# Attention's scores and P V as plain fp32 products, late q^T ranked behind the first heads, and new durations in the planner

## The chip, the cores and the metric

One core of a Trainium2 chip runs the whole model in one launch. The metric is device time in microseconds. Engines are named as in the profile: PE (matrix products; PEld is its weight load), DVE (vector), ACT (scalar, activations), POOL (gpsimd), and SP, the queue from which all DMAs of this kernel are issued.

## The reference, cut to what matters

A two-layer encoder on 512 tokens of width 1024, all fp32. Each sub-layer modulates its input with a shift and a scale that are linear in silu(c), runs a mixer or an MLP, and ends in a layer norm. The change lies in the first sub-layer, attention:

```python
h = x * (1.0 + scale) + shift
qkv = h @ w_in                      # 8 query heads, 2 key/value heads, 128 wide
q, k = rope(q[..., :32]), rope(k[..., :32])   # the first 32 of 128 features are rotated
# per block of 128 queries: keys of the block before, the own and the next
scores = einsum("bnqhgd,bnjhd->bnhgqj", qb, kb) * HEAD_DIM ** -0.5
m = max(max(scores), sink)
p = exp(scores - m)                 # outside the window: 0
probs = p / (sum(p) + exp(sink - m))
o = einsum("bnhgqj,bnjhd->bnqhgd", probs, vb)
y = o @ w_out
x = layer_norm(ALPHA * x + (1.0 + gate) * y)
```

After it come MLP 0, a recurrent block (depthwise convolution, gates, scans in both directions), and MLP 1, each with its layer norm.

## The kernel before, in words

**Products.** A large product is three products of a faster 32-bit type (fp32r): both operands are split into a high and a low part, and mm3 (L632) issues high x high, high x low, low x high. split (L639) makes the parts of an activation: ACT writes the high part, DVE subtracts it from the source (L642). Weights come by DMA as units of 128 x 1024 into one of four raw buffers and are split into one of six w buffers (conv_unit, L582). A few small products are not split: the transposes of P and of the layer norm's output, and the sums over partitions by a matrix of ones (L763), which are plain fp32 products.

**Stages.** k^T and q^T of six heads are accumulated over eight weight units (L1103 to L1114); rope (L990) evacuates them, four at a time: ACT packs the 32 rows that are rotated, each of the four tiles is split, DVE shuffles, multiplies and adds the packed rows, the result is split too, and two DMAs per head put the rotated rows back (L1009). V follows (L1129). Then the heads, in the order 0, 5, 1, 2, 3, 4, 6, 7 (L1017). For a head (L1166) there are four score blocks of 128 queries against 256 or 384 keys (L1175); DVE adds the mask and takes the maximum (L1178), ACT exponentiates, DVE or ACT divides (L1206), PE transposes P, the transposed P is split (put, L1198), and four products make P V (L1218), which is split again for the output projection. The q^T of heads 6 and 7 (48 products) is made after the heads at places 1 and 3 (LP, L1226). The output projection goes over two halves of 512 features (fh 0 and 1), out_tiles (L903); its first half starts as soon as heads are done, and with the second half each block of 128 tokens gets its layer norm (ln_block, L812) and is transposed for the MLP, whose first products (five units) take the first two blocks alone (NS, L680).

**Background.** The shifts, scales and gates of later sub-layers are matrix-vector products that DVE does as running sums, `acc = raw * sc + acc` over 128 x 1024 (gemv_tasks, L752), eight to a vector, with a plain product by ones at the end. Three vectors, 24 sums, fall into attention. Their weights go through the same four raw buffers, of which two are kept for them at least (keep_raw, L1117). Lines BV, BH and BG of the parameters say how many such tasks are recorded after a piece of V, after a head, and after a late head.

**What sets the order.** The kernel is first recorded as a list of operations. price (L293) gives each a duration, and schedule (L330) simulates five engines with these durations, always letting an engine take the ready operation of the lowest rank. The rank is the place in the recording plus an offset (later, L703, and the parameters CO, BO, PO, VO and others). The result is a fixed order of instructions on each engine, in which each engine then runs, waiting by semaphores. A duration in price has thus no effect but on the order.

The planner's price of PE (L303), of DVE (L308) and of DMA (L317 and L445), rope, attn and the parameter table are what the diff touches.

Of the kernel before, what the change touches and what calls it, by code (L numbers as in the profile page):

```python
# [233 lines left out]
class Program:  # L234
# [58 lines left out]
    def price(self, op, reads, writes):  # L293
# [7 lines left out]
        if op.eng == "tensor":  # L301
            op.nbytes = n * (reads[0].p1 - reads[0].p0) / 128
            passes = 1 if op.fn == "transpose" or op.kw["rhs"].ops[-1][0] == "b" else 4  # L303
            op.cost = 109 if op.fn == "transpose" else max(107 if passes == 1 else 213, passes * n * 0.4167 + 16)
# [3 lines left out]
        elif op.eng == "vector":  # L308
            if op.fn == "bn_stats":
                op.cost = reads[0].shape[1] * 1.042 + 68  # L310
            elif op.fn in ("tensor_scalar", "tensor_copy") and not ps:
                op.cost = n * 0.52 + 69 + 60 * aps
            else:
                op.cost = n * 1.042 + 65 + (60 if aps else 0)
        elif op.eng == "gpsimd":
            op.cost = {"memset": n * 0.85, "tensor_scalar": n * 3.4 + 105, "partition_all_reduce": n * 7.0}.get(op.fn, n * 2.105 + 147)
        else:  # L317
            p = w.shape[0]
            op.nbytes = p * n * 4
            op.cost = 480 if any(v.tile.kind == "dr" for v in reads + writes) or not reads else 650  # L320
# [9 lines left out]
    def schedule(self):  # L330
# [36 lines left out]
        while len(order) < total:  # L367
# [156 lines left out]
class Kernel:  # L524
# [127 lines left out]
    def fill(self):  # L652
# [16 lines left out]
        BH=4,  # L669
        BG=6,  # L670
# [15 lines left out]
        RP=60,  # L686
# [3 lines left out]
        LP=(1, 3),  # L690
        RE=0,
# [298 lines left out]
    def rope(self, heads):  # L990
# [5 lines left out]
        ph, pl = self.ex[10][:n, :], self.ex[11][:n, :]  # L996
# [5 lines left out]
        e = nc.gpsimd if self.P["RE"] else v  # L1002
        e.tensor_tensor(out=pk, in0=pk, in1=cos, op=ALU.mult)
# [3 lines left out]
        for i, (p, hi, lo) in enumerate(heads):  # L1007
            for dst, src in ((hi, self.ex[10]), (lo, self.ex[11])):
                nc.sync.dma_start(out=dst[0:32, :].bitcast(F32), in_=src[32 * i : 32 * i + 32, :])  # L1009

    def attn(self):
# [14 lines left out]
        def KTt(kv, lo, hi):  # L1026
            return self.HID(4 + kv, lo, hi)

        def V(t, lo, hi):
            return hid[12 + t][:, lo:hi].bitcast(F32R), hid[12 + t][:, 256 + lo : 256 + hi].bitcast(F32R)  # L1030

        def Q(h, lo, hi):
            if h == 5:
                return self.HID(3, lo, hi)
            a = self.ex[2 * (h % 6)], self.ex[2 * (h % 6) + 1]
# [505 lines left out]
```

## Time and profile before

| | |
|---|---|
| three runs | 1210.86, 1211.11, 1212.65 us (median 1211.11) |
| the profiled execution's own time | 1211.31 us |
| its span, first to last instruction | 1209.5 us |
| PE busy | 1142.6 us, 94% |
| DVE busy | 872.3 us, 72% |
| ACT busy | 528.5 us, 44% |
| PE's granted clock, mean | 0.974 |

A clock of 1.00 is 2.4 GHz; the lower of its two levels is 1.2 GHz, so a stretch with 0.50 ran at the lower one throughout. All operations of this kernel stand under one line, L476, since the planner issues them; so they are told apart by the names of their tiles: ps a PSUM bank, raw and w weights before and after the split, ht the transposed activations, hid and ex and xb and rows and acc working tiles. `rows<-raw,sc,rows` and `acc<-raw,sc,acc` are the running sums of the background. In the timeline a row merges instructions of one kind that follow each other; a start-to-start distance says how long the engine was held, which is a little less than an instruction's own duration.

### The profile page before, as it was taken

How to read it: one execution, taken by the hardware profiler on the slowest of the kernel's cores; microseconds unless marked ns; L12 is line 12 of the kernel's file. 1: busy time of each engine (PE TensorE's matmuls, PEld its weight loads, DVE VectorE, ACT ScalarE, POOL GpSimd, SP SyncE). 2: the span in 40 equal slices, each digit the busy share in tenths (PEclk: the TensorE clock that was granted, in tenths of full speed). 3: DMA queues.
4: the chain of work that ended last, by engine and by line, in shares of the span. 5: the costliest groups of instructions: out<-in, count | busy, mean ns of one | idle time of the engine just before them, and what ended most of it. 6: DMA issues, size and time to landing. Idle time of an engine off the chain costs nothing.

```text
span 1209.5 us, 14406 instructions
## 1 busy us (share of the span) xinstructions
PE 1142.6 (94%) x5332; PEld 942.0 (78%) x5332; DVE 872.3 (72%) x1303; ACT 528.5 (44%) x787; POOL 77.0 (6%) x47
## 2 busy tenths in 40 slices
PE   7977989999999899999999989979999999999996
PEld 5876858988888688887887877768888888888885
DVE  7899979978878885449958788689935444444447
ACT  4465654512322342324378889834531322322311
POOL 1000000022232220000000000000000000000004
PEclk9998999999999999999999989989999999999998
DMA  9866552367667753321333542442532323232201
GB/s 351 288 201 202 166 188 71 121 211 263 207 234 236 244 196 135 95 97 37 100 101 100 142 125 83 150 140 86 169 111 89 103 90 103 90 101 90 101 1 70
DMA packets 54140, 172.01 MB, mean 142 GB/s; under 512 B 7715, under 2 KB 8227, under 8 KB 54070
## 3 DMA queue, kind: packets, MB, share of 16 engines
q1 hardware_dynamic: 54070, 171.09, 43.1%
q8 instruction: 42, 0.69, 0.2%
q14 instruction: 28, 0.23, 0.1%
HBM read 160.56 MB, written 2.11 MB: 134 GB/s over the span
## 4 chain that ended last, share of the span: by engine, by line
PE 57%; DVE 20%; ACT 8%; DMA 8%; issue 5%; POOL 2%; SPq 1%; DVEq 0%; ACTq 0%; POOLq 0%
PE ps L476 57%; DVE ex L476 5%; DVE w L476 5%; DVE rows L476 4%; DMA raw<-in_adaw 3%; DVE xb L476 2%; ACT rows L476 2%; ACT w L476 2%; POOL ex L476 2%; DMA raw<-in_W 1%; DMA rows<-w 1%; DVE ht L476 1%; DVE acc L476 1%; ACT ex L476 1%; ACT L476 1%
## 5 line engine op out<-in xcount | busy, mean ns | idle before, releaser
L476 PE MATMUL ps<-ht,w 128*128 128x512 f32 (+1 forms) x2664 | 557.1, 371 | 6.3 <-ACT w L476 3.9
L476 PEld LDWEIGHTS ps<-ht,w 128*128 128x128 f32 x2664 | 464.2, 191 | 94.6 <-ACT w L476 4.3
L476 PE MATMUL ps<-w,hid 128*128 128x512 f32 (+1 forms) x1800 | 415.2, 390 | 0.0
L476 DVE TENSOR_TENSOR w<-raw,w 128x1024 fp32r<-128x1024 f32 x192 | 241.0, 1260 | 223.1 <-ACT w L476 220.7
L476 PEld LDWEIGHTS ps<-w,hid 128*128 128x128 f32 x1800 | 335.3, 188 | 72.0 <-DVE rows L476 0.2
L476 ACT CAST w<-raw 128x1024 fp32r<-128x1024 f32 x192 | 198.5, 1041 | 420.6 <-PE ps L476 305.2
L476 PE MATMUL ps<-w,ht 128*128 128x512 f32 (+1 forms) x336 | 76.0, 378 | 6.9 <-DVE w L476 3.6
L476 PEld LDWEIGHTS ps<-w,ht 128*128 128x128 f32 x336 | 58.4, 197 | 19.4 <-DVE w L476 4.1
L476 DVE SCALAR_TENSOR_TENSOR ex<-rows,ps 128x512 f32<-128x512 f32 (+1 forms) x81 | 53.3, 674 | 20.4 <-PE ps L476 20.4
L476 DVE SCALAR_TENSOR_TENSOR acc<-raw,sc,acc 128x1024 f32<-128x1024 f32 x40 | 52.8, 1320 | 16.4 <-DMA raw<-in_adaw 16.1
L476 DVE SCALAR_TENSOR_TENSOR rows<-raw,sc,rows 128x1024 f32<-128x1024 f32 x40 | 54.6, 1365 | 5.7 <-DMA raw<-in_adaw 5.5
L476 ACT ACTIVATE rows<-ps 128x512 f32<-128x512 f32 x66 | 39.2, 593 | 44.6 <-PE ps L476 41.7
L476 DVE TENSOR_TENSOR xb<-xb,ex 128x512 f32<-128x512 f32 (+1 forms) x81 | 55.9, 703 | 0.6
L476 POOL TENSOR_TENSOR ex<-xb,rows 128x512 f32<-128x512 f32 x5 | 6.8, 1375 | 750.7 <-ACT xb L476 750.7
L476 DVE TENSOR_TENSOR hid<-ex,hid 128x512 fp32r<-128x512 f32 x66 | 47.6, 722 | 5.3 <-ACT hid L476 0.7
L476 DVE TENSOR_TENSOR ex<-rows 128x512 f32<-128x512 f32 x64 | 46.0, 718 | 4.8 <-ACT rows L476 4.7
L476 ACT ACTIVATE hid<-rows 128x512 fp32r<-128x512 f32 x64 | 40.5, 633 | 1.9
L476 PE MATMUL ps<-ex,w 96*128 96x512 f32 x108 | 33.1, 464 | 7.7 <-ACT w L476 4.2
L476 PEld LDWEIGHTS ps<-ex,w 96*128 96x128 f32 x108 | 23.5, 223 | 15.7 <-ACT w L476 5.8
L476 DVE TENSOR_TENSOR rows<-rows,ex 128x512 f32<-128x512 f32 x32 | 21.4, 688 | 19.6 <-DMA rows<-rows 12.5
L476 ACT ACTIVATE xb<-xb,mv 128x512 f32<-128x512 f32 x29 | 22.2, 809 | 26.4 <-DVE mv L476 26.3
L476 ACT ACT_TABLE_LOAD x24 | 30.8, 1283 | 1.1 <-PEq L1533 0.7
(147 smaller groups left out, 819.3 us busy)
## 6 DMA issues: line engine op xcount, KB each, us to landing
raw<-in_W SPq DMA_DIRECT2D x184, 512.0 KB
raw<-in_adaw SPq DMA_DIRECT2D x80, 512.0 KB
ex<-in_ada0t SPq DMA_DIRECT2D x28, 256.0 KB
rows<-w SPq DMA_DIRECT2D x16, 192.0 KB
raw<-in_W SPq DMA_DIRECT2D x8, 288.0 KB
rows<-rows SPq DMA_DIRECT2D x36, 64.0 KB
xb<-in_xT SPq DMA_DIRECT2D x8, 256.0 KB
rows<-in_lnb SPq DMA_DIRECT2D x4, 512.0 KB
```

The lines of the kernel that those rows point to most:

```text
L476: op.ins = getattr(getattr(nc, op.eng), op.fn)(*args, **kw)
```

## The change

Scores and P V become one plain fp32 product each. q^T, k^T, V and the transposed P are no longer split but copied from PSUM, by ACT or DVE as the strings QE and PE say; the rotated rows are not split either, and one DMA per head puts them back instead of two. The q^T of heads 6 and 7 is recorded before all heads, with 200 added to its rank (QP), and the places LP are gone. Three background tasks are recorded after every head (BH). The P tiles of successive heads use two halves of the same buffers. The planner's prices change: a plain product counts its four passes as activity of PE, a scan costs 2.083 ns a column instead of 1.042, a DMA's issue is 600 ns for all, its data come at 330 bytes per ns instead of 360, and up to 5000 ns of them may be queued instead of 3000.

```diff
             passes = 1 if op.fn == "transpose" or op.kw["rhs"].ops[-1][0] == "b" else 4
-            op.nbytes = n * (reads[0].p1 - reads[0].p0) / 128
+            op.nbytes = passes * n * (reads[0].p1 - reads[0].p0) / 128
...
+            elif op.fn == "tensor_tensor_scan":
+                op.cost = n * 2.083 + 65
...
-            op.cost = 480 if any(v.tile.kind == "dr" for v in reads + writes) or not reads else 650
+            op.cost = 600
...
-                b = max(st + op.cost + 720, dma_free)
-                dma_free = b + op.nbytes / 360.0
-                now[e] = max(st + op.cost, dma_free - 3000)
-                op.end = dma_free
+                b = max(st + 1030, dma_free)
+                dma_free = b + op.nbytes / 330.0
+                now[e] = max(st + op.cost, dma_free - 5000)
+                op.end = dma_free + (30 if op.nbytes > 300000 else -230)
...
-        BH=4,
-        BG=6,
+        BH=3,
+        QE='aavavavava',
+        PE='ava',
...
+        VP=0,
+        QP=200,
-        LP=(1, 3),
...
-        for p, hi, lo in heads:
-            self.split(p[:, :], hi, lo)
+        for i, (p, dst) in enumerate(heads):
+            if how[i] == "a":
+                nc.scalar.copy(out=dst, in_=p[:, :])
+            else:
+                v.tensor_copy(out=dst, in_=p[:, :])
...
-        self.split(pk, ph.bitcast(F32R), pl.bitcast(F32R))
-        for i, (p, hi, lo) in enumerate(heads):
-            for dst, src in ((hi, self.ex[10]), (lo, self.ex[11])):
-                nc.sync.dma_start(out=dst[0:32, :].bitcast(F32), in_=src[32 * i : 32 * i + 32, :])
+        for i, (p, dst) in enumerate(heads):
+            nc.sync.dma_start(out=dst[0:32, :], in_=self.rows[4][32 * i : 32 * i + 32, 0:512])
...
-                self.split(p[:, 0:256], *V(t, 0, 256))
+                nc.scalar.copy(out=V(t, 0, 256), in_=p[:, 0:256])
...
+        self.nc.offset += self.P["QP"]
+        for n in range(2):
+            u = N_WQ + 2 + n
+            self.prep(u, ahead=2)
+            p = self.ps()
+            for k in range(KT):
+                self.mm3(p[:, :], self.W(u, k * 128, k * 128 + 128), self.HT(k), k == 0, k == KT - 1)
...
-                self.mm3(p[:, :n], Q(h, b * 128, b * 128 + 128), KTt(kv, lo, hi), True, True)
+                nc.tensor.matmul(p[:, :n], lhsT=Q(h, b * 128, b * 128 + 128), rhs=KTt(kv, lo, hi), start=True, stop=True)
...
-                    self.split(pj[j][:, :n], hi, lo)
+                    if self.P["PE"][min(j, 2)] == "a":
+                        nc.scalar.copy(out=PT(h, j, n), in_=pj[j][:, :n])
+                    else:
+                        v.tensor_copy(out=PT(h, j, n), in_=pj[j][:, :n])
...
-                self.mm3(o[:, q0 : q0 + cnt], V(j, kv * 128, kv * 128 + 128), PT(h, j, cnt), n == 0, n == 3)
+                nc.tensor.matmul(
+                    o[:, q0 : q0 + cnt], lhsT=V(j, kv * 128, kv * 128 + 128), rhs=PT(h, j, cnt), start=n == 0, stop=n == 3, skip_group_check=True
+                )
```

Because the planner rules on all engines, the order moves almost everywhere in attention. Three places matter. The rows are the program's, L476 (before) or L478 (after) being the line that issues everything, and a number behind a name telling tiles apart.

On PE, after V, before: the last score block of the first head (three products), then the late q^T of head 6 in one piece (w_93), and the next head's scores; the first transpose stands some 30 rows further on.

```order
L476 MATMUL ps_709<-hid_108,ex_527 128x256
L476 MATMUL ps_709<-hid_109,ex_527 128x256
L476 MATMUL ps_709<-hid_108,ex_536 128x256
L476 MATMUL ps_714<-ht,w_93 128x512 x24
L476 MATMUL ps_758<-hid_108,ex_532 128x256
L476 MATMUL ps_758<-hid_109,ex_532 128x256
```

The same place after: the scores of the first two heads and more stand ahead, one row to a block, and the late q^T is cut into pieces between which the first transposes (ident) stand.

```order
L478 MATMUL ps_723<-hid_109,ex_555 128x256
L478 MATMUL ps_726<-hid_108,ex_540 128x256
L478 MATMUL ps_733<-ht,w_93 128x512 x10
L478 MATMUL ps_756<-hid_108,ex_524 128x256
L478 MATMUL ps_760<-ident,xb_705 128x128
L478 MATMUL ps_733<-ht,w_93 128x512
L478 MATMUL ps_760<-ident,rows 128x128
L478 MATMUL ps_760<-ident,ex_81 128x128
```

So the 24 products of a late q^T moved from in front of the second head's scores into the time in which the first heads' softmax runs.

On DVE, at the end of the second head's score reductions, before: the sums of the background (raw, sc) stand between the small softmax operations (den, nm, rd) and the normalizations of the first head.

```order
L476 SCALAR_TENSOR_TENSOR rows<-raw_85,sc,rows 128x1024
L476 TENSOR_TENSOR den_796<-den_796,es_777 128x4
L476 TENSOR_SCALAR nm_826<-mx_788 128x4
L476 SCALAR_TENSOR_TENSOR rows<-raw_86,sc,rows 128x1024
L476 RECIPROCAL rd_835<-den_796 128x4
L476 SCALAR_TENSOR_TENSOR rows<-raw_87,sc,rows 128x1024
L476 TENSOR_SCALAR xb_732<-xb_732,rd_835 128x256
L476 TENSOR_SCALAR ex_81<-ex_81,rd_835 128x384
L476 TENSOR_TENSOR den_832<-den_832,es_830 128x4
L476 SCALAR_TENSOR_TENSOR rows<-raw_85,sc,rows 128x1024
L476 RECIPROCAL rd_856<-den_832 128x4
L476 TENSOR_TENSOR w_93<-raw_84,w_93 128x1024
```

The same place after; the COPY is a P tile out of PSUM.

```order
L478 TENSOR_SCALAR nm_731<-mx_716 128x4
L478 TENSOR_TENSOR den_729<-den_729,es_721 128x4
L478 RECIPROCAL rd_751<-den_729 128x4
L478 TENSOR_SCALAR xb_705<-xb_705,rd_751 128x256
L478 TENSOR_SCALAR ex_81<-ex_81,rd_751 128x384
L478 ISA xb_705,mx_778<-ps_688,rows,sinks 128x256
L478 ISA mx_778 128x1
L478 COPY xb_319<-ps_774 128x384
L478 TENSOR_TENSOR den_748<-den_748,es_744 128x4
```

The sums moved behind: four of the 24 stand before the first reduction, none between there and the fourth head's P copy, the others after it.

On DVE, around the last P V's split (ht from ps), before: the operations that build the layer norm's rows (rows from rows or acc, 128x1024) and the last splits, then the evacuation of the output projection (ex from rows, ps).

```order
L476 TENSOR_TENSOR w_91<-raw_84,w_91 128x1024
L476 SCALAR_TENSOR_TENSOR rows<-rows 128x1024
L476 TENSOR_TENSOR xb_879<-ps_1441,xb_879 128x384
L476 TENSOR_TENSOR rows<-acc_68,rows 128x1024
L476 TENSOR_TENSOR ht<-ps_1460,ht 128x512
L476 TENSOR_TENSOR ht<-ps_1477,ht 128x384
```

After, from the last split on:

```order
L478 TENSOR_TENSOR ht<-ps_1301,ht 128x512
L478 SCALAR_TENSOR_TENSOR ex_1326<-rows,ps_987 128x512
L478 SCALAR_TENSOR_TENSOR rows<-raw_85,sc,rows 128x1024
L478 SCALAR_TENSOR_TENSOR ex_1337<-rows,ps_993 128x512
L478 SCALAR_TENSOR_TENSOR rows<-raw_84,sc,rows 128x1024
L478 TENSOR_TENSOR xb_1306<-xb_1306,ex_1337 128x512
```

Four sums and all three row operations now stand behind the last split, among the evacuations; and on PE the eight transposes of the first block's layer norm, which stood among the output projection's last products, stand behind them all.

## Rows read from the trace of the kernel before

**Rows 1.** The page: PE's busy time, share of the span, instructions.

```profile
PE 1142.6 (94%) x5332; PEld 942.0 (78%) x5332; DVE 872.3 (72%) x1303; ACT 528.5 (44%) x787; POOL 77.0 (6%) x47
```

**Rows 2.** The table by stretches: attention in three, then the MLP's first products.

```profile
core 0: us, PE busy (x) PEld busy (x) DVE busy (x) ACT busy (x) POOL busy (x), PEclk, DMA share, GB/s
56.39:98.11 41.72, 29.69 (x188) 25.93 (x187) 38.06 (x71) 25.87 (x53) 0.00 (x0) 0.88 0.64 208
98.11:169.43 71.32, 64.82 (x331) 51.60 (x331) 61.56 (x133) 46.44 (x111) 2.46 (x4) 0.97 0.59 194
169.43:200.87 31.44, 29.36 (x133) 22.95 (x131) 28.13 (x59) 14.52 (x20) 0.00 (x0) 1.00 0.18 55
200.87:206.60 5.73, 5.73 (x35) 5.63 (x35) 5.73 (x14) 2.07 (x3) 0.00 (x0) 0.70 0.23 70
206.60:214.00 7.40, 7.40 (x65) 7.38 (x64) 7.40 (x16) 1.75 (x4) 0.00 (x0) 1.00 0.35 122
```

**Rows 3.** Timeline of PE: start, length, operation, idle before and its releaser.

```profile
59.11 11.07 PE L476 MATMUL ps<-w,ht 128*128 128x256 f32 x96
...
72.49 1.44 PE L476 MATMUL ps<-hid,ex 128*128 128x256 f32 x8 [1.72 <-DMA ex<-ex]
73.77 5.67 PE L476 MATMUL ps<-ht,w 128*128 128x512 f32 x24
...
88.56 0.48 PE L476 MATMUL ps<-ident,rows 128*128 128x128 f32 x1 [4.16 <-ACT rows L476]
...
98.11 3.86 PE L476 MATMUL ps<-xb,hid 128*128 128x512 f32 x12 [0.78 <-DVE mx L476]
...
169.43 2.04 PE L476 MATMUL ps<-w,ht 128*128 128x512 f32 x8
...
199.54 1.26 PE L476 MATMUL ps<-ident,ex 128*128 128x128 f32 x8 [1.40 <-DVE ex L476]
```

**Rows 4.** Timeline of DVE from the first head's reductions to the first P V.

```profile
78.84 0.16 DVE L476 TENSOR_SCALAR nm<-mx 128x4 f32<-128x4 f32 x1
...
83.49 1.28 DVE L476 SCALAR_TENSOR_TENSOR rows<-raw,sc,rows 128x1024 f32<-128x1024 f32 x1 [0.65 <-DMA raw<-in_adaw]
84.69 0.48 DVE L476 CUSTOM_DVE_ANT_0 xb<-ps,rows,sinks 128x256 f32<-128x256 f32 x1
...
92.32 1.20 DVE L476 TENSOR_TENSOR w<-raw,w 128x1024 fp32r<-128x1024 f32 x1
93.43 0.68 DVE L476 TENSOR_TENSOR xb<-ps,xb 128x512 fp32r<-128x512 f32 x1
94.03 1.28 DVE L476 SCALAR_TENSOR_TENSOR rows<-raw,sc,rows 128x1024 f32<-128x1024 f32 x1
...
95.49 0.42 DVE L476 TENSOR_SCALAR rows<-rows,rd 128x384 f32<-128x384 f32 x1
95.82 0.55 DVE L476 TENSOR_TENSOR xb<-ps,xb 128x384 fp32r<-128x384 f32 x1
96.28 1.28 DVE L476 SCALAR_TENSOR_TENSOR acc<-raw,sc,acc 128x1024 f32<-128x1024 f32 x1
```

**Rows 5.** Chain of waits in 76:100: start, length, what.

```profile
78.64 4.82 DMA raw<-in_adaw
...
86.40 4.54 DMA raw<-in_adaw
```

**Rows 6.** PE's weight loads of a plain fp32 product (sum over partitions).

```profile
102.37 0.19 PEld L476 LDWEIGHTS ps<-rows,ones 128*128 128x128 f32 x1 [0.27 <-DVE mx L476]
102.80 0.19 PEld L476 LDWEIGHTS ps<-rows,ones 128*128 128x128 f32 x1 [0.24 <-issue]
```

**Rows 7.** Timeline of DVE: the second block's layer norm output.

```profile
198.80 1.29 DVE L476 TENSOR_TENSOR ex<-ex,rows 128x512 f32<-128x512 f32 x2
```

**Rows 8.** The recurrent stage: one stretch, and its scans by form.

```profile
600.00:860.00 260.00, 243.62 (x1073) 197.55 (x1072) 208.69 (x308) 183.37 (x268) 0.00 (x0) 0.95 0.39 118
...
L476 DVE TENSOR_TENSOR_SCAN w<-rows 128x512 f32<-128x512 f32 x16 | 19.1, 1215 | 0.0
```

More of the change, by code (lines that the diff above doesn't have):

```diff
@@ L689 @@
         RO=0,
-        LP=(1, 3),
-        RE=0,
         KW=(0, 0, 1),
@@ L988, in late_consts, with rope @@
         nc.sync.dma_start(out=self.ex[12][:, 0:384], in_=I["mask"])
-    def rope(self, heads):
+    def rope(self, heads, how):
         nc, v = self.nc, self.nc.vector
@@ L1118, in attn @@
         self.modes = self.P["AM"]
-        qk = [(tiles[m], *(KTt(m, 0, 512) if m < 2 else Q(m - 2, 0, 512))) for m in range(8)]
-        self.rope(qk[:4])
-        self.rope(qk[4:])
+        qk = [(tiles[m], KTt(m, 0, 512) if m < 2 else Q(m - 2, 0, 512)) for m in range(8)]
+        self.rope(qk[:4], self.P["QE"][:4])
+        self.rope(qk[4:], self.P["QE"][4:8])
         accv, r = self.acc2, [a[:, :] for a in self.rows]
@@ L1135, in attn @@
             with self.later("VO"):
-                self.split(p[:, 0:256], *V(t, 0, 256))
+                nc.scalar.copy(out=V(t, 0, 256), in_=p[:, 0:256])
+        self.nc.offset -= self.P["VP"]
+        for t in range(TB):
             self.bg(self.P["BV"])
@@ L1139, in attn @@
         self.done(u + 1)
+        late = []
+        self.nc.offset += self.P["QP"]
[5 more added lines that the diff above has]
+                self.mm3(p[:, :], self.W(u, k * 128, k * 128 + 128), self.HT(k), k == 0, k == KT - 1)
+            self.done(u)
+            late.append((p, Q(6 + n, 0, 512)))
+        self.rope(late, self.P["QE"][8:])
+        self.nc.offset -= self.P["QP"]
         self.renew("xb", range(TB))
-        pt_at = [(0, 0, 512), (1, 0, 512), (2, 0, 384), (0, 256, 768)]
+        pt_at = [(0, 0), (1, 0), (2, 0), (0, 256)]
         pt_n = [256, 384, 384, 256]
@@ L1147, in PT @@
         def PT(h, j, n):
-            t, hi, lo = pt_at[j]
-            i = order.index(h)
-            if i > 3 and i % 2:
-                hi, lo = 4096 + t * 1024 + hi, 4096 + t * 1024 + lo
-                return self.ht[:, hi : hi + n].bitcast(F32R), self.ht[:, lo : lo + n].bitcast(F32R)
-            return self.xb[t][:, hi : hi + n].bitcast(F32R), self.xb[t][:, lo : lo + n].bitcast(F32R)
+            t, a = pt_at[j]
+            a += order.index(h) % 2 * 512
+            return self.xb[t][:, a : a + n]
         n_s = [0]
@@ L1222, in attn @@
         uo = N_WQ + 4
-        late, at = [], self.P["LP"]
-        for i, h in enumerate(order):
+        for h in order:
             head(h)
-            if i in at:
-                n = at.index(i)
-                u = N_WQ + 2 + n
-                self.prep(u, ahead=2)
-                p = self.ps()
-                for k in range(KT):
-                    self.mm3(p[:, :], self.W(u, k * 128, k * 128 + 128), self.HT(k), k == 0, k == KT - 1)
-                self.done(u)
-                late.append((p, *Q(6 + n, 0, 512)))
-            self.bg(self.P["BH" if i <= at[1] else "BG"])
-            if i == at[1]:
-                assert 4 * self.P["BV"] + (i + 1) * self.P["BH"] <= 20
-                with self.later("RP"):
-                    self.rope(late)
-                for half in range(2):
-                    nc.gpsimd.memset(self.ht[:, 5120 + half * 512 + 384 : 5120 + half * 512 + 512], 0.0)
+            self.bg(self.P["BH"])
         self.load_ln_rows(0)
@@ L1247, in attn @@
         self.renew("ex", range(10))
+        self.renew("hid", range(8, 16))
         self.flush_bg()
```

18 lines of the change are left out of this document (6 added, 12 removed).

## The prediction

> **What bounds the kernel now.** I read the page first: PE is busy for 94% of the span [rows 1], so a saving has to come from the few stretches in which PE waits. The table by stretches then shows where these are. In 56.39:98.11 us (V, the first scores, the first softmax) PE is busy for 29.69 of 41.72 us and DVE for 38.06; in 98.11:169.43 (the rest of the heads) PE for 64.82 and DVE for 61.56 of 71.32 us; in 169.43:200.87 (the rest of the output projection and the layer norm) PE for 29.36 and DVE for 28.13 of 31.44 us [rows 2]. So in attention DVE is as full as PE, and in its first third it is what PE waits for. The timeline of PE shows the holes: 4.16 us in front of the first transpose at 88.56, and the first P V product only at 98.11, 28 us after V was done [rows 3]. The timeline of DVE shows why: between the score reductions and the normalizations stand sums of the background matrix-vector work (raw times sc into rows or acc), 1.20 us each, and the split of P [rows 4]. The chain of waits adds a second reason: in 76:100 two of these sums wait 4.82 and 4.54 us for their 512 KB of raw weights [rows 5], because only two or three raw buffers circulate. What stands behind such a sum on DVE waits with it.
>
> **PE: what the plain products cost.** A plain fp32 product is not unknown here: the sums over partitions (rows, ones) are such products. Their weight loads stand 0.43 us apart and there are two to a product [rows 6], so 512 columns take 0.86 us, 1.68 ns a column. Three split passes take 3 x 11.07/96 us on 256 columns, 1.35 ns a column, and 3 x 5.67/24 on 512, at most 1.38 [rows 3]. A head has 256+384+384+256 = 1280 columns of scores and 512+384+256+256 = 1408 of P V; eight heads have 21,504. The change costs PE 21,504 x 0.30 to 0.37 ns = 6.5 to 8.0 us; I take 7.5. All of it is PE's own time; whether it lengthens the stage depends on the holes.
>
> **DVE: what goes.** Starts in [rows 4] give 0.60 us for a split of 512 columns (93.43 to 94.03), 0.46 for 384 (95.82 to 96.28), and by their ratio 0.34 for 256. Gone are 18 of 512 (ten q^T and k^T, one per head for P), 16 of 384 (two per head), 4 of 256 (V) and the three of the rotated rows (0.60): 10.8 + 7.4 + 1.4 + 1.8 = 21.4 us. New are DVE copies out of PSUM, 4 of 512 and 8 of 384. No copy of that kind is in the trace; the bounds are the split's price (2.4 + 3.7 = 6.1 us) and that of a one-input operation in SBUF, 0.33 us for 384 (95.49 to 95.82), 4.4 us in all. I take 6.1, the row that also reads PSUM. DVE loses 15.3 us. The Trainium skill (VectorE: DVE Perf Modes, Why PSUM operands drop a tier) says that an fp32 operation with a PSUM operand runs at one element per cycle, which speaks against hoping for the faster price; by it the sum would be this same 6.1 us, and no run so far shows it. ScalarE does one P copy less per head and six of ten q and k copies instead of ten casts; it was busy for 72 of 113 us [rows 2] and stays behind the other two. The rope writes halve from 20 small DMAs to 10, so q of head 0 arrives before V is done: the 1.7 us hole in front of the scores goes.
>
> **The order: the first four heads.** In the new DVE order no matrix-vector sum stands between the first score reduction and the fourth head's P copy (between the same points there were 13 before), and on PE the products of the late q^T stand in the hole after the scores. I walk through the new order with these prices. V ends at 70.2 as before. Scores of head 0 take 2.15 us and are reduced by 74.6. Before, 9.7 us passed from there (78.84, nm from mx) to the first transpose at 88.56, with three sums of 1.20 us and a wait of 0.65 in between [rows 3, 4]; without these it is 5.4 us, so the transposes start at 80 and the first P V at about 83 (98.11). From there PE is full: V 11.1, four heads at 2.15 + 2.37 us = 18.1, both late q^T 2 x 5.4 = 10.7 and 40 transposes at 0.13 = 5.2 [rows 3] make 45.1 us, so P V of the fourth head ends at 59.1 + 45.1 = 104. Of the 41.72 us up to the first P V, PE was idle for 12.0 [rows 2]: this is the cover under which the dearer products disappear; without it they cost their 7.5 us.
>
> **The order: the last four heads.** What DVE skipped early comes now: 16 sums between the fourth head's P copy and the last head's split. The last twelve of these run through two raw buffers alone (raw_84 and raw_85 in the order). One turn is a reload of 4.4 us [rows 5] and the sum's 1.20, 5.6 us for two sums. DVE needs about 15 us from 106 for two heads' reductions, the rope of the late heads (2.5), two weight splits (2.2) and three sums, plus some 2 us for its first reload, so the run of twelve sums begins at about 121; five turns later, at 149, its last pair starts, and the last head's split ends at 153, its P V at 151. PE alone could be there at 148 (before: 169.4): 59.1 + V 11.1 + eight heads 36.2 + late q^T 10.7 + 80 transposes 10.4 + 72 products of the output projection 17 + four sums over partitions 3.4 = 147.9. Bounds: 148 (PE never waits) and 158 (PE as idle as in 98.11:169.43, 6.5 us, and the walk too short by as much again).
>
> **The tail.** Before, 31.4 us passed from the last P V to the first MLP product at 200.87 [rows 2, 3]; PE had 28 us of output projection there, and the second block's layer norm ended at 200.0 [rows 7]. Now DVE has, between the last split and the same point, 32 operations of 512 columns (19.2 us), four sums that used to be done before (4.8), the three operations that build the layer norm's rows (two of them were done before) and four weight splits (7 x 1.11 = 7.8) and small ones (1.5): 33.3 us, and about 4 us of waits, for the last reloads (four loads of x and the norm's rows now stand in the same queue) and for the last sum's product, which PE has behind the second block's output products. So the second block is ready at 153 + 37.3 = 190.2 and the MLP starts at 191, while PE finished at 181 and waits for 8 us in two pieces. I add 0.5 for small waits: 191.5. The stage gains 200.87 - 191.5 = 9.4 us.
>
> **After it.** PE comes out of a wait of 4 to 5 us. Before, after 1.4 us of idle, its first 5.73 us ran at a clock of 0.70 [rows 2]; I add 1 us for 0.50 over the same stretch (5.73 x 0.20 = 1.1). The Trainium skill (TensorE: Matmul & The Clock Gate, HAM oscillation) says that each wait for data between bursts lets PE fall to the lower clock and that the next burst starts slow; the 0.70 agrees, and by that rule too the wait would cost about the same 1 us on top. Elsewhere the same instructions run in a slightly other order. The planner priced a scan at 512 x 1.042 + 65 = 598 ns; the trace has 1215 [rows 8], and the corrected formula gives 1131. In the recurrent stage, 600:860, PE is idle for 16.4 us [rows 8]. Its new order can win or lose there; nothing in the trace prices it, so the bounds are half of that idle time either way, 8 us; the MLP stretches are full and keep their length. I take a gain of 1.
>
> **Sum.** Profiled execution 1211.31 us (span 1209.5, 1.8 around it; 0.2 above the median of 1211.11): 1211.3 - 9.4 + 1 - 1 = 1202.
>
> **Rivals.**
> PE-bound to the end: the raw buffers keep up, the last P V ends at 148 and the tail is as short as before, MLP at 148 + 31.4 = 179.4: 1211.3 - 21.5 = 1190. For it: PE's sum. Against it: 4.4 us per reload in the chain of waits, and four more sums in the tail. Chance 0.13.
> The tail eats it: the waits behind the reloads are longer than in my walk, 6 to 8 us more, so that the MLP starts at 198 to 200: 1208 to 1211. For it: a walk leaves out small waits, and DVE was 88% busy in the heads before [rows 2]. Chance 0.13.
> Slower: the plain products decide. If the softmax chain (reduction, exponential, sum, normalization, transpose) and not DVE's load set the holes, they stay, and PE's 7.5 us go on top: 1219. It decides from the point where the first P V is not earlier than about 95. For it: PE was 91% busy in 98.11:169.43 [rows 2]. Against it: the waits in 76:100 are for DVE and the raw loads, and both go. Chance 0.11.
> That the orders elsewhere turn against it by more than 8 us I give 0.03 (no change).
>
> **The numbers.** The forecast has 0.60, its own range is 1196 to 1208. The range for 8 in 10 reaches into both neighbours: 1189 to 1212. What a measurement can tell from no change here is 0.2%, 2.4 us. Faster: 0.60 + 0.13 + 0.09 of the tail's case = 0.82; same: 0.04 + 0.03 = 0.07; slower 0.11.
>
> **What would show it.** In the profile after: the first transposes at about 80 and the first P V at about 83; DVE without matrix-vector sums from 73 to 104 and waiting for raw loads from 105 on; two PE instructions per score block, 0.43 us apart for 512 columns; the last P V at 151; PE idle twice before the first MLP product at 191.5; from there to the end of the span 1008 to 1009 us (before: 1209.5 - 200.87 = 1008.6). It is wrong if P V of the first head comes after 90, if PE has no idle time in front of the MLP, or if the stretch from the MLP's start to the end differs by more than 8 us.

## The result, and the profile after

The change takes 1199.61 us (median of 4 runs, 1197.29 to 1201.10) against 1210.98 (4 runs of the kernel before on the same chip): ratio 0.9902, 95% interval [0.9883, 0.9921]. Forecast 1202, faster. The profiled execution took 1198.96 us, its span 1197.2.

The page of the kernel after, its first line (before: [rows 1]):

```profile
PE 1138.4 (95%) x5268; PEld 931.5 (78%) x5268; DVE 858.1 (72%) x1274; ACT 523.1 (44%) x774; POOL 77.5 (6%) x45
```

The table by stretches of the kernel after: from V to the first P V, to the end of the last P V, to the first MLP product, and the first 5.67 us of the MLP. It answers to the same marks in [rows 2], which stand there at 98.11, 169.43 and 200.87; the first stretch there begins at 56.39, 2.7 us ahead of V.

```profile
59.90:89.87 29.97, 25.39 (x150) 21.18 (x149) 22.22 (x47) 17.87 (x40) 0.00 (x0) 0.94 0.60 192
89.87:157.69 67.82, 66.00 (x285) 46.68 (x284) 52.76 (x119) 39.65 (x100) 0.95 (x1) 1.00 0.52 162
157.69:197.93 40.24, 32.88 (x142) 25.21 (x140) 35.76 (x67) 20.23 (x26) 0.96 (x1) 0.97 0.52 175
197.93:203.60 5.67, 5.67 (x33) 5.67 (x33) 5.67 (x17) 2.41 (x4) 0.00 (x0) 0.62 0.27 82
```

Heads are dense now (PE 66.00 of 67.82 us), but the tail grew to 40.24, and of 11.7 us gained up to the last P V only 2.9 are left at the first MLP product. The whole of V to MLP, before and after:

```profile
59.11:200.87 141.76, 121.16 (x637) 98.24 (x635) 125.53 (x258) 84.16 (x180) 2.46 (x4) 0.95 0.52 168
```
```profile
59.90:197.93 138.03, 124.28 (x574) 93.08 (x572) 110.74 (x232) 77.74 (x166) 1.91 (x2) 0.98 0.54 172
```

DVE, the third engine of the row, is busy for 14.8 us less (I had 15.3); its idle time went from 16.2 to 27.3 us. The timeline of PE after, at the places of [rows 3]: the hole in front of the last scores of heads 0 and 1, the first transpose, the first and the last P V, a wait behind it, two in front of the MLP, the MLP.

```profile
79.78 4.31 PE L478 MATMUL ps<-hid,ex 128*128 128x256 f32 x10 [4.54 <-DMA ex<-rows]
...
86.67 0.27 PE L478 MATMUL ps<-ident,xb 128*128 128x128 f32 x1
...
89.87 2.53 PE L478 MATMUL ps<-xb,hid 128*128 128x512 f32 x8
...
155.06 2.63 PE L478 MATMUL ps<-xb,hid 128*128 128x512 f32 x8
157.35 1.51 PE L478 MATMUL ps<-w,ht 128*128 128x512 f32 x5
160.59 4.72 PE L478 MATMUL ps<-w,ht 128*128 128x512 f32 x19 [1.73 <-ACT ht L478]
...
190.53 1.26 PE L478 MATMUL ps<-ident,ex 128*128 128x128 f32 x8 [1.27 <-DVE ex L478]
196.14 1.97 PE L478 MATMUL ps<-ident,ex 128*128 128x128 f32 x8 [4.35 <-DVE ex L478]
197.93 5.27 PE L478 MATMUL ps<-ht,w 128*128 128x256 f32 x26
```

So where did the rest come from? Stage by stage, by marks of PE's timeline (us; "LN" is the first transposes of the layer norm in front of the recurrent stage, the next mark its first gate product, then its first output product, then the last transposes in front of the second MLP; "rest" ends with PE's last product):

| | to MLP start | MLP to LN | LN to gates | recurrent | its output | rest |
|---|---|---|---|---|---|---|
| before | 200.87 | 355.96 | 54.15 | 149.00 | 97.45 | 340.28 |
| after | 197.93 | 350.95 | 55.33 | 142.99 | 97.95 | 340.25 |
| difference | -2.94 | -5.01 | +1.18 | -6.01 | +0.50 | -0.03 |

Three quarters of the gain (9.4 of the span's 12.3 us) lie outside attention, where I had put a loss of 1 us and a gain of 1. In the first MLP a wait is gone (before, then after):

```profile
415.14 17.98 PE L476 MATMUL ps<-ht,w 128*128 128x512 f32 x68 [3.86 <-ACT w L476]
```
```profile
409.09 15.86 PE L478 MATMUL ps<-ht,w 128*128 128x512 f32 x68 [0.36 <-DVE w L478]
```

There the weights of the MLP and those of the background sums share SP's queue; in the recurrent stage the order of DVE and ACT around the scans differs. Both, I thought, hang on the planner's durations and on nothing that attention computes. That is the theory to test (T): the corrected durations make the gain behind the MLP's start, and attention makes 2.9 us. Its rival (R): attention leaves another phase behind it, and the later stages profit from that.

### The profile page after: what moved, and what is told of

Its sections match the earlier page's. It is cut to its first block, busy times and chain, and to the rows that moved or that the text cites. A ratio compares the mean times of both kernels' runs of the same rounds, so it can differ in the third digit from the quotient of the medians.

```text
span 1197.2 us, 14220 instructions
## 1 busy us (share of the span) xinstructions
PE 1138.4 (95%) x5268; PEld 931.5 (78%) x5268; DVE 858.1 (72%) x1274; ACT 523.1 (44%) x774; POOL 77.5 (6%) x45
## 4 chain that ended last, share of the span: by engine, by line
PE 68%; DVE 14%; ACT 9%; DMA 6%; issue 3%; SPq 0%; DVEq 0%; ACTq 0%
PE ps L478 68%; DVE ex L478 4%; DVE w L478 3%; ACT w L478 3%; ACT rows L478 2%; DVE rows L478 2%; DMA raw<-in_adaw 2%; DVE xb L478 2%; ACT L478 1%; DMA rows<-w 1%; ACT ex L478 1%; DVE acc L478 1%; DMA rows<-rows 1%; DVE ht L478 1%; DVE mv L478 1%
## 5 line engine op out<-in xcount | busy, mean ns | idle before, releaser
L478 PE MATMUL ps<-ht,w 128*128 128x512 f32 (+1 forms) x2664 | 557.6, 370 | 2.2 <-ACT ht L478 1.8
L478 PEld LDWEIGHTS ps<-ht,w 128*128 128x128 f32 x2664 | 462.1, 191 | 89.2 <-ACT ht L478 2.9
L478 PE MATMUL ps<-w,hid 128*128 128x512 f32 (+1 forms) x1800 | 413.7, 389 | 1.4 <-ACT w L478 1.4
L478 DVE TENSOR_TENSOR w<-raw,w 128x1024 fp32r<-128x1024 f32 x192 | 241.2, 1262 | 214.3 <-ACT w L478 212.8
L478 PEld LDWEIGHTS ps<-w,hid 128*128 128x128 f32 x1800 | 334.3, 188 | 74.9 <-ACT w L478 1.8
L478 ACT CAST w<-raw 128x1024 fp32r<-128x1024 f32 x192 | 198.4, 1042 | 403.7 <-PE ps L478 303.1
L478 PE MATMUL ps<-w,ht 128*128 128x512 f32 (+1 forms) x336 | 76.1, 378 | 9.6 <-DVE w L478 5.7
L478 PEld LDWEIGHTS ps<-w,ht 128*128 128x128 f32 x336 | 58.0, 195 | 22.8 <-DVE w L478 6.2
L478 DVE SCALAR_TENSOR_TENSOR ex<-rows,ps 128x512 f32<-128x512 f32 (+1 forms) x81 | 53.2, 673 | 17.3 <-PE ps L478 17.2
L478 ACT ACTIVATE rows<-ps 128x512 f32<-128x512 f32 x66 | 39.2, 594 | 58.8 <-PE ps L478 58.8
L478 DVE SCALAR_TENSOR_TENSOR acc<-raw,sc,acc 128x1024 f32<-128x1024 f32 x40 | 54.0, 1350 | 15.1 <-DMA raw<-in_adaw 14.6
L478 DVE SCALAR_TENSOR_TENSOR rows<-raw,sc,rows 128x1024 f32<-128x1024 f32 x40 | 54.4, 1361 | 13.1 <-DMA raw<-in_adaw 12.9
L478 DVE TENSOR_TENSOR xb<-xb,ex 128x512 f32<-128x512 f32 (+1 forms) x81 | 56.0, 704 | 0.7
L478 POOL TENSOR_TENSOR ex<-xb,rows 128x512 f32<-128x512 f32 x5 | 6.8, 1385 | 740.6 <-ACT xb L478 739.1
L478 DVE TENSOR_TENSOR ex<-rows 128x512 f32<-128x512 f32 x64 | 47.5, 743 | 2.7 <-ACT rows L478 2.7
L478 DVE TENSOR_TENSOR hid<-ex,hid 128x512 fp32r<-128x512 f32 x66 | 45.5, 691 | 5.1 <-ACT hid L478 0.3
L478 ACT ACTIVATE hid<-rows 128x512 fp32r<-128x512 f32 x64 | 40.5, 633 | 1.9
L478 PE MATMUL ps<-ident,ex 128*128 128x128 f32 x124 | 21.1, 295 | 14.4 <-DVE ex L478 14.4
L478 DVE TENSOR_TENSOR rows<-rows,ex 128x512 f32<-128x512 f32 x32 | 21.4, 688 | 18.1 <-DMA rows<-rows 12.0
L478 ACT ACTIVATE xb<-xb,mv 128x512 f32<-128x512 f32 x29 | 22.2, 808 | 24.4 <-DVE mv L478 24.4
L478 PE MATMUL ps<-ex,w 96*128 96x512 f32 x108 | 28.6, 419 | 2.7 <-ACT w L478 1.5
```

The costliest lines, as they stand in the source:

```text
L478: op.ins = getattr(getattr(nc, op.eng), op.fn)(*args, **kw)
```

## The experiments

Marks in one table (us; "w" is PE's wait for a weight in the first MLP, 190 us or more behind its start; a wait of 1.2 to 1.4 us some 125 us behind it, in all but before and e2, is not in it; the medians are of 4 to 12 runs; the kernel before beside them had 1209.9 to 1211.8):

| | median | ratio to before | MLP start | w | recurrent | its output |
|---|---|---|---|---|---|---|
| before | 1210.98 | | 200.87 | 4.5 | 149.00 | 97.45 |
| after | 1199.61 | 0.9902 [0.9883, 0.9921] | 197.93 | 0.4 | 142.99 | 97.95 |
| e1 before, all durations | 1201.86 | 0.9922 [0.9908, 0.9936] | 195.90 | 3.4 | 141.45 | 98.58 |
| e2 after, old durations | 1224.64 | 1.0113 [1.0097, 1.0128] | 213.76 | 3.5 | 148.77 | 97.12 |
| e3 after, old scan | 1207.94 | 0.9975 [0.9963, 0.9986] | 197.03 | 0.0 | 150.72 | 96.34 |
| e4 after, old DMA | 1202.32 | 0.9926 [0.9906, 0.9946] | 199.32 | 8.9 | 144.73 | 91.16 |
| e5 after, old activity | 1210.90 | 0.9995 [0.9984, 1.0007] | 207.34 | 0.0 | 143.67 | 97.42 |
| e6 before, DMA alone | 1216.80 | 1.0043 [1.0026, 1.0059] | 202.86 | 3.2 | 149.75 | 97.24 |
| e7 no early sums | 1215.77 | 1.0036 [1.0022, 1.0049] | 205.63 | 0.5 | 142.82 | 97.92 |
| e8 four sums a head | 1229.58 | 1.0148 [1.0132, 1.0165] | 232.31 | 0.0 | 141.52 | 97.97 |
| e9 before, scan + activity | 1200.33 | 0.9918 [0.9904, 0.9932] | 198.55 | 6.3 | 143.62 | 90.19 |
| e10 eight early sums | 1215.38 | 1.0041 [1.0027, 1.0054] | 207.55 | 3.8 | 143.83 | 96.89 |
| e11 quarter loads | 1194.77 | 0.9874 [0.9856, 0.9892] | 192.36 | 1.2 | 142.56 | 96.31 |
| e12 old DMA from the recurrent stage on | 1197.65 | 0.9887 [0.9868, 0.9906] | 200.90 | 0.0 | 143.93 | 90.82 |

How far one profile can be trusted: after, e3 and e12 have the same order up to the end of the first MLP, and their MLP starts at 197.93, 197.03 and 200.90. So a mark of one profile is good to some 4 us. A length between two marks is better known: from the MLP's start to the layer norm the same three take 350.95, 350.22 and 350.30. The marks are those of the profiled execution, which in e3 took 1203.90 us and in e4 1206.35, each 4 us off its median. The intervals of the ratios are some 2 us to either side.

**e1 and e2: the two halves apart.** e1 is the kernel before with the diff's hunks in `price` and `schedule`, e2 the kernel after without them.

```diff
-            op.nbytes = n * (reads[0].p1 - reads[0].p0) / 128
+            op.nbytes = passes * n * (reads[0].p1 - reads[0].p0) / 128
...
+            elif op.fn == "tensor_tensor_scan":
+                op.cost = n * 2.083 + 65
...
+            op.cost = 600
...
+                dma_free = b + op.nbytes / 330.0
...
```

> The kernel before with only the planner's corrected durations (scan, DMA, DMA issue, PE activity); products, copies and parameters of attention as before. Theory T (the 9.3 us gained behind the MLP's start come from the later stages' order, which the corrected durations change): from the first MLP product to the end 999 to 1001 us, the stretch from there to the fifth burst of w,hid 226 to 228 us (before 232.1), the recurrent stage from its first gate product to its first output product 142 to 145 us (before 149.0); MLP start near before's 200.9 (199 to 203), time 1200 to 1204. Rival R (the later stages gain because attention leaves other buffers and another phase behind, whatever the prices): 1007 to 1009 us behind the MLP's start, time 1208 to 1212.

> The changed kernel with the planner's old durations (scan, DMA, issue, PE activity): attention's plain products, copies and new order alone. Theory T: the MLP starts at 196 to 200, from there to the end 1007 to 1009 us, recurrent stage 148 to 150 us, time 1206 to 1209. Rival R: 999 to 1001 us behind the MLP's start, time 1198 to 1201.

Measured: e1 1201.86, e2 1224.64 us. For the recurrent stage rival R falls: the durations alone, on the old attention, give 141.45 there, and 8.9 of the 11.4 us of the total. For the first MLP it does not fall. From the MLP's start to the layer norm e1 takes 355.97 us, as long as before (355.96), and e2 354.15; with both halves it is 350.95. So behind the MLP's start e1 takes 1002.6 us and not 999 to 1001, and it gains 5.0 us in front of it, which T did not have. My own half of T falls as well. Attention's products, copies and ranks under the old durations do not gain 3 us, they lose 14: the MLP starts at 213.76. Under the corrected ones they are worth 1201.86 to 1199.61, two intervals that overlap: no difference that these runs can tell.

**e3, e4, e5, e6, e9: which duration does what.** e3, e4 and e5 take one correction out of the kernel after (scan; DMA and its issue; PE's activity); e6 and e9 put one or two into the kernel before. The edits are single hunks of the diff above.

> The changed kernel with the scan priced at 598 ns as before and all other durations corrected. If the scan's price makes the recurrent stage's gain (my first guess): that stage 148 to 150 us rather than 143.0, the rest as in the changed kernel, time 1204 to 1207. Rival (the DMA's price makes it): recurrent stage 143 to 144, time 1199 to 1201.

> The changed kernel with the DMA priced as before (360 bytes per ns, 720 ns, no offset at its end, issue 480 or 650 ns), the scan's price corrected. If the DMA's price makes the gain in the first MLP (the matrix-vector sums and weights share one queue there): first MLP product to fifth burst of w,hid 231 to 233 us rather than 226.9, recurrent stage still 143 to 145, time 1203 to 1206. Rival (that gain is the scan's too, or chance in the queue): 226 to 228, time 1199 to 1201.

> The changed kernel with one of the planner's corrections taken back: PE's activity counted as columns and not as passes times columns (the planner then holds PE for slow during the plain products). Attention alone under all old prices lost 12.9 us up to the MLP's start, and neither the old scan price nor the old DMA price does that here. Theory A (the activity makes that loss): the MLP starts at 208 to 215, the sums all stand ahead of the first output tiles' evacuation, from the MLP's start to the end 998 to 1001, time 1209 to 1216. Rival (only all old prices together lose it): MLP start 197 to 200, time 1198 to 1203.

> The kernel before with the corrected DMA durations alone. With all corrections it gained 5.0 us up to the MLP's start and 7.5 in the recurrent stage. Theory T: the first is the DMA price's, the second the scan's, so the MLP starts at 195 to 197, the recurrent stage stays at 148 to 150 us, time 1204 to 1208. Rival (the first is the PE activity's or chance): MLP start 199 to 202, time 1208 to 1212.

> The kernel before with two corrections, the scan's price and PE's activity, the DMA priced as before. All corrections together moved the MLP's start from 200.9 to 195.9 and took 7.5 us from the recurrent stage; the DMA's alone gave neither (202.9, 149.8). Theory T: the activity moves attention and the scan's price the recurrent stage, so MLP start 195 to 197, recurrent stage 141 to 144, time 1200 to 1204. Rival (attention's part needs the DMA price beside it): MLP start 200 to 203, recurrent stage 141 to 144, time 1203 to 1207.

The scan's price makes the recurrent stage. It is 149 to 151 us in every kernel with the old price and 141 to 145 in every one with the new, and e3 loses 8.3 us in the median (expected 1204 to 1207; 1207.94). The table by stretches for that stage, after and e3:

```profile
604.21:747.20 142.99, 137.06 (x578) 109.98 (x577) 119.09 (x162) 128.25 (x191) 0.00 (x0) 0.98 0.38 112
```
```profile
601.67:752.39 150.72, 140.84 (x578) 112.49 (x576) 121.84 (x166) 129.09 (x191) 0.00 (x0) 0.94 0.36 106
```

The same products: PE is idle for 5.9 us and the clock stands at 0.98; in e3 it is idle for 9.9 at 0.94. So the worse order is paid twice, with 4.0 us of idle time and with 3.8 us more of busy time for the same 578 products. e9 has the old attention and the old DMA price, and its 1200.33 us cannot be told from the kernel after: the prices of the scan and of PE's activity are enough for the gain.

The DMA's price moves the wait w in the first MLP, but not alone. It is 3.5 to 8.9 us in the four kernels with the old price and 0 to 1.2 in seven of the ten with the new. In e1, e6 and e10 PE waits 3.2 to 3.8 us as well, for another split some 30 us further on; e6, then e10:

```profile
445.52 4.70 PE L476 MATMUL ps<-w,hid 128*128 128x512 f32 x13 [3.21 <-DVE w L476]
```
```profile
451.07 32.99 PE L478 MATMUL ps<-w,hid 128*128 128x512 f32 x136 [3.77 <-DVE w L478]
```

So the old attention has nothing from the new price in this stage: 355.43 us in e6, 355.96 before. The length of the stage follows PE's idle time; before, then after:

```profile
200.87:556.83 355.96, 351.16 (x1638) 292.33 (x1639) 269.39 (x321) 112.41 (x143) 54.33 (x20) 0.99 0.54 178
```
```profile
197.93:548.88 350.95, 349.21 (x1638) 291.19 (x1638) 269.92 (x319) 112.36 (x143) 55.61 (x20) 0.99 0.55 180
```

PE is idle for 4.80 us of it before and for 1.74 after, which is 3.06 of the 5.01 us; the other 1.95 are busy time of the same 1638 products.

The new price also costs the output projection of the recurrent stage some 7 us when the scan's price is right (96 to 99 against 90 to 91), so that the two nearly cancel: e4's median is only 2.7 us above after, with intervals that overlap. The waits of PE for weights there, e4 in the MLP, then the kernel after in the output projection:

```profile
PE ps L478 <- ACT w L478: 8.9, 1, 8.9
```
```profile
797.07 20.21 PE L478 MATMUL ps<-w,ht 128*128 128x512 f32 x74 [5.72 <-DVE w L478]
```

PE's activity is what the plain products need. With the old count (e5) the planner holds PE for slow beside them, prices the next products at double, and orders the last heads' work differently; the last P V waits for a P copy that stands on DVE behind two sums, which wait 1.45 and 0.66 us for their weights. PE's timeline of e5, then DVE's:

```profile
162.04 5.06 PE L478 MATMUL ps<-xb,hid 128*128 128x512 f32 x8 [4.28 <-DVE xb L478]
```
```profile
157.68 1.28 DVE L478 SCALAR_TENSOR_TENSOR rows<-raw,sc,rows 128x1024 f32<-128x1024 f32 x1 [1.45 <-DMA raw<-in_adaw]
158.88 0.68 DVE L478 TENSOR_TENSOR ht<-ps,ht 128x512 fp32r<-128x512 f32 x1
160.23 1.28 DVE L478 SCALAR_TENSOR_TENSOR rows<-raw,sc,rows 128x1024 f32<-128x1024 f32 x1 [0.66 <-DMA raw<-in_adaw]
161.43 0.55 DVE L478 COPY xb<-ps 128x384 f32<-128x384 f32 x1
```

e5 costs 11.3 us, as expected under theory A (1210.90; MLP start 207.34, a little below its range). In the kernel before, whose attention has almost no plain products, e6 (without it) starts its MLP at 202.86 and e9 (with it) at 198.55; e6 is slower than before by 0.43%, which neither theory had. Up to the MLP these differences are as small as one profile's spread, so which correction moves the old attention stays open.

**e7, e8, e10: the sums ahead of the first heads.**

```diff
-        BV=1,
+        BV=0,      # e7, e8; e10: BV=2
-        BH=3,
+        BH=4,      # e8 alone
```

> The changed kernel without the four matrix-vector sums between V and the first head (BV 0): they come later. The step of my walk that failed was the second half of the rope, late behind the first of these sums, which waited 2.00 us for its raw weights. Theory W (that wait makes the 4.54 us hole of PE at 79.8): the hole shrinks below 1.5 us, the first P V comes at 82 to 86 (changed kernel 89.9). For the end: if DVE's later load decides, the sums come back in the tail and the MLP starts at 197 to 200, time 1199 to 1202; if PE's earlier start carries through, at 192 to 195, time 1194 to 1197.

> As the one before, and four sums a head in program order rather than three, so that all of them stand ahead of the first evacuation of the output projection and none in the tail. If DVE's load in the tail bounds the MLP's start: tail 33 to 37 us rather than 40.2, MLP start 190 to 195, time 1193 to 1197. Rival (the ring of raw buffers bounds the sums, so the heads wait instead): last P V at 162 to 168, MLP start 197 to 202, time 1199 to 1204.

> The changed kernel with eight matrix-vector sums between V and the heads in program order rather than four (BV 2); the planner then puts four of them among the first two heads and none behind the first evacuation. Taking the early four away cost 7.7 us up to the MLP's start. If the raw ring is what bounds the sums, using it from the start pays: tail 32 to 36 us, MLP start 192 to 196, time 1194 to 1198. Rival (the sums in the first two heads hold the first P V up as in the kernel before): first P V after 92, MLP start 198 to 203, time 1200 to 1206.

Theory W (the first sum's wait makes PE's hole) falls. Without the early sums the hole is 2.31 us, but the first P V comes at 88.65, not at 82 to 86: the second half of the rope is as late as in the kernel after. The sum in front of it was not what it waited for. What the sums did hold are the first head's reductions, which begin at 75.95 in e7 and at 79.74 after. ScalarE's timeline says what the rope waited for: the kernel before, after, and e7, the packing of the last four heads' rows.

```profile
65.47 2.38 ACT L476 COPY rows<-ps 32x512 f32<-32x512 f32 x4 [0.76 <-DVE ex L476]
```
```profile
68.50 2.38 ACT L478 COPY rows<-ps 32x512 f32<-32x512 f32 x4 [2.37 <-DMA hid<-rows]
```
```profile
68.57 2.37 ACT L478 COPY rows<-ps 32x512 f32<-32x512 f32 x4 [2.68 <-DMA hid<-rows]
```

Before, the rotated rows went out from two split buffers, and the packing buffer was free as soon as DVE had read it. Now the DMAs read the packing buffer itself, so the second packing waits until they have landed. The chain of waits after has that step too:

```profile
65.13 3.26 DMA hid<-rows
```

That this wait makes the first P V late is not shown. No run gives the packing another buffer, and in e4 the planner packs two and two, the last ends at 67.83 (before 67.85), PE waits for no DMA of the rope, and the first P V still comes at 90.27. ScalarE and PE of e4:

```profile
66.65 1.18 ACT L478 COPY rows<-ps 32x512 f32<-32x512 f32 x2
```
```profile
76.84 2.53 PE L478 MATMUL ps<-hid,ex 128*128 128x256 f32 x8 [1.30 <-DVE mx L478]
...
90.27 4.30 PE L478 MATMUL ps<-xb,hid 128*128 128x512 f32 x8
```

All three kernels are slower than after and than every range given for them. In e7 PE stands for 9.36 us at a product of a sum that is not ready; e8 has two such waits, 17.8 and 9.2 us, and its tail did not shrink (41.1 us). e10's tail did (34.7 us), but its first P V came at 96.41, as its rival has it, and its last at 172.87. PE of e7:

```profile
134.21 2.07 PE L478 MATMUL ps<-rows,ones 128*128 128x512 f32 x2 [9.36 <-DVE rows L478]
```

**e11: the raw weights themselves.**

```diff
+                    q = 256 if (idx, part) in ((0, 2), (1, 1), (1, 0)) else D
...
-                        out=self.raw[r][:, :], in_=self.I["adaw"][idx, k * 128 : (k + 1) * 128, part * D : (part + 1) * D]
+                        out=self.raw[r][:, :q], in_=self.I["adaw"][idx, k * 128 : (k + 1) * 128, part * D : part * D + q]
```

> The changed kernel in the same order, but the raw weights of attention's matrix-vector sums are loaded only in their first quarter of columns (128 KB rather than 512), so these sums work on incomplete weights and the modulation rows come out other; the planner prices the loads as before. Theory R (the ring of raw buffers takes back what DVE saved): DVE's waits for raw loads between V and the MLP fall from 9.8 us to under 2, the MLP starts at 186 to 193, time 1188 to 1195. Rival (the order and the softmax chain hold it, not the loads): MLP start 195 to 198, time 1197 to 1200.

Theory R of this run (the ring, that is the raw buffers that are refilled in turn, takes back what DVE saved) holds, at its weak end. The kernel leaves out three quarters of these weights, so it is a test and no version. The waits of DVE for raw weights between V and the MLP, after, then e11:

```profile
DVE rows L478 <- DMA raw<-in_adaw: 7.7, 8, 2.4
...
DVE acc L478 <- DMA raw<-in_adaw: 2.1, 3, 1.3
```
```profile
DVE rows L478 <- DMA raw<-in_adaw: 1.5, 2, 1.1
```

Of 9.8 us of waiting 8.3 go, the MLP starts at 192.36 (5.6 us earlier than after, a little more than one profile's spread) and the median falls by 4.8 us; the two intervals still touch. In the same order and with the loads out of the way the tail is still 38.70 us, and PE still waits 4.35 us at its end: that part is DVE's work.

**e12: a version from the experiments.** The DMA's corrected price up to the end of the first MLP, the old one behind it.

```diff
+                if op.old:
...
+                    dma_free = b + op.nbytes / 360.0
...
+        self.nc.old = True
         self.rnn(self.P["NS"][1])
```

> The changed kernel with the corrected DMA durations up to the end of the first MLP, and the old ones from the recurrent stage on; its order is the changed kernel's up to there. Two runs with the old DMA price and the corrected scan price had an output projection of the recurrent stage of 90.2 and 91.2 us, four with the corrected DMA price 97 to 98.6, where PE waits 5.72 us for a weight split. If that order is the cause: output projection 90 to 92 us, recurrent stage 143 to 145, up to it as in the changed kernel, time 1192 to 1196. Rival (chance of the profiled runs): output projection 96 to 99, time 1198 to 1201.

The output projection is 90.82 us, as expected; the time, 1197.65, is not (1192 to 1196). It is the fastest median of those that compute everything, but its interval [0.9868, 0.9906] overlaps that of the kernel after. In its profile the MLP starts 3 us later than after in the same order, and the last stage is 3 us longer.

## Why the forecast was right, and where it was not

The total was right, 2.4 us from the forecast, and the sum behind it was not: up to the MLP's start I had -9.4 us for a measured -2.9, behind it +1 - 1 = 0 for -9.3. The two errors, 6.5 and 9.3 us, have opposite signs: that the total came out is luck.

- **PE's price of plain products.** Right. One head's P V takes 2.37 us (92.24 - 89.87 in PE's timeline), as I had it; two heads' scores 4.12 us (111.41 to 115.53), where I had 4.30. The upper price of 0.37 ns a column does not come out of its rows (1.68 - 1.35 is 0.33, or 7.1 us in all). PE's busy time from V to the MLP rose by 3.1 us only, while the granted clock rose from 0.95 to 0.98.
- **DVE's saving.** Right: 14.8 for 15.3. A 384-column copy out of PSUM holds DVE for 0.47 us (88.98 to 89.45), the dear one of my two bounds. The Trainium skill (VectorE: DVE Perf Modes, Why PSUM operands drop a tier) says that an operand in PSUM keeps fp32 at the slowest mode; this row agrees:

```profile
88.98 0.55 DVE L478 COPY xb<-ps 128x384 f32<-128x384 f32 x1
89.45 0.15 DVE L478 TENSOR_TENSOR den<-den,es 128x4 f32<-128x4 f32 x1
```

- **The first four heads.** This step failed: "Scores of head 0 take 2.15 us and are reduced by 74.6". The scores did begin right behind V, at 71.21, and from the maxima to the first transpose it was 4.65 us (82.02 to 86.67) for my 5.4. But the reductions began at 79.74 and were done at 82.02 (nm), 7.4 us late, because DVE had the four early sums, the second half of the rope and two weight splits ahead of them, which the walk left out:

```profile
68.24 1.29 DVE L478 SCALAR_TENSOR_TENSOR rows<-raw,sc,rows 128x1024 f32<-128x1024 f32 x1 [2.00 <-DMA raw<-in_adaw]
...
78.54 1.29 DVE L478 SCALAR_TENSOR_TENSOR rows<-raw,sc,rows 128x1024 f32<-128x1024 f32 x1 [0.30 <-DMA raw<-in_adaw]
79.74 0.48 DVE L478 CUSTOM_DVE_ANT_0 xb<-ps,rows,sinks 128x256 f32<-128x256 f32 x1
...
82.02 0.17 DVE L478 TENSOR_SCALAR nm<-mx 128x4 f32<-128x4 f32 x1
```

PE was late by itself too: its hole ended at 79.78, with a DMA of the rope, and 6.9 us of further scores and late q^T stand in its order ahead of the first transpose. I had counted that the rope's DMAs are halved and not that they now read the packing buffer, which held the next packing up for 2.37 us. As both ways end close to 86.67, taking from one moves the first P V little: by 1.2 us in e7 (no early sums), not at all in e4 (the packing early). What each is worth stays open. P V of the first head came at 89.87 for 83; by my own words the forecast "is wrong if P V of the first head comes after 90", and it came 0.13 us before that.
- **The last four heads.** The ring was right in kind: DVE's waits for raw loads from V to the MLP are 9.8 us, and e11 prices them at some 5 us. Its first sign was misread: 4.82 and 4.54 us in [rows 5] are the lengths of two transfers, and no sum waited that long. In the kernel before, all these waits of DVE were 2.5 us:

```profile
DVE rows L476 <- DMA raw<-in_adaw: 2.1, 4, 0.8
...
DVE acc L476 <- DMA raw<-in_adaw: 0.4, 1, 0.4
```

P V of the fourth head ended at 111 (104), the last at 157.7 (151): the 7 us of the first heads carried through.
- **The tail.** Right: 40.2 us; the prediction's 151 to 191.5 is 40.5. PE waits twice at its end, 1.27 and 4.35 us, 5.6 rather than 8.
- **MLP start.** 197.93 for 191.5, a gain of 2.9 for 9.4, all of the miss from the first heads. The rival "the tail eats it" (198 to 200) described this better than the likeliest case did, though by another mechanism.
- **After it.** 0.62 over 5.67 us, where I had 0.50 over 5.73 in place of 0.70: a loss of 0.08 x 5.67 = 0.5 us for 1.
- **Orders elsewhere.** This term was mis-sized: -1 with bounds of 8 either way; from the MLP's start to the end of the span it was -9.3 (1008.6 to 999.3), outside the 8 us beyond which the forecast was to count as wrong. I saw that the planner priced a scan at 598 ns for 1215 and did not follow it: the stage's idle time, 16.4 us, was the size of what a better order could give, and e3 shows 7.7 us of it in the stage. The DMA correction I did not price at all; with the new attention beside it the first MLP is 5.0 us shorter.
- **What the change is.** The prediction credited attention. e1 and e2 show the opposite: the corrected durations are worth 9 us without it; it is worth -14 us without them, and nothing that these runs can tell with them. The rival "slower", 1219 for products that do not hide, was close to what e2 does (1224.64), but not by its mechanism: in e2 the first P V comes early, at 84.15, and the heads and the tail behind it lose.

## What to carry to other kernels

Where a planner orders the instructions, its durations are part of the program: a change to them and a change to the work must be timed apart, and an edit that looks like a loss may be one only under wrong prices. When a step is shortened, ask of each DMA in it which buffer it reads and who writes that buffer next. And time taken off an engine counts only as far as the transfers that feed it keep up: here 14.8 us less work on DVE became 11 us more idle time, 7.3 of them waits for raw weights.

## What the runs showed of the hardware

PE's clock carried more of the difference than I had expected, and after short waits too. The 144 products of the recurrent stage's input behind the layer norm, before (after a wait of 1.24 us) and after (1.73 us):

```profile
585.71:610.98 25.27, 25.27 (x145) 22.05 (x145) 18.70 (x25) 9.88 (x14) 0.00 (x0) 1.00 0.41 132
```
```profile
577.57:604.21 26.64, 26.64 (x144) 23.53 (x145) 18.71 (x25) 9.88 (x14) 0.00 (x0) 0.94 0.38 125
```

The same dense stretch takes 1.4 us longer at a granted clock of 0.94. How long the last wait was does not decide it: e10 ran these products at 1.00 after 2.71 us, e4 at 0.94 after 1.39. e10, then e4:

```profile
592.30 1.32 PE L478 MATMUL ps<-ident,ex 128*128 128x128 f32 x8 [2.71 <-DVE ex L478]
```
```profile
593.64:619.46 25.82, 25.61 (x145) 22.16 (x146) 17.75 (x24) 9.88 (x14) 0.00 (x0) 1.00 0.35 109
```
```profile
587.16 1.32 PE L478 MATMUL ps<-ident,ex 128*128 128x128 f32 x8 [1.39 <-DVE ex L478]
```
```profile
588.49:615.12 26.63, 26.63 (x144) 23.48 (x145) 18.72 (x25) 9.88 (x14) 0.00 (x0) 0.94 0.39 125
```

Of the fourteen kernels seven ran this stretch at 1.00 (after waits of 1.24 to 2.71 us) and seven at 0.94 or 0.95 (after 1.39 to 2.23); what decides stays open. The Trainium skill (TensorE: Matmul & The Clock Gate, HAM oscillation) tells of a kernel in which each wait for DMA between bursts lets PE fall to the lower clock, so that the next burst starts slow. 0.62 behind the 4.35 us in front of the MLP agrees, and so does 0.70 behind 1.40 us there before [rows 2, 3]; the seven stretches at 1.00 show that not every wait of this length does it.
